# One core, one stream of tokens: the feed-forward layers with hi and lo of x in one 512-column product

## The chip, the cores and the metric

The program runs on one core of a Trainium2 chip. The metric is the device time of one execution in microseconds, the median of several. A core has five engines that work side by side: TensorE (PE) multiplies matrices, VectorE (DVE) and ScalarE (ACT) do element-wise work, GpSimd (POOL) does some more of it, and SyncE (SP) issues most DMA transfers. TensorE's clock has two levels, 1.2 and 2.4 GHz; the profile's "granted clock" is its share of the higher one.

## The reference

Two transformer blocks run one after the other on 256 tokens of width 1024, all in float32. Each has two layers. What the change touches are the feed-forward parts, four in block 1 and one or two in each layer of block 2:

```python
def rmsnorm(x, g):
    xf = x.astype(F32)
    y = xf * lax.rsqrt(jnp.mean(xf * xf, axis=-1, keepdims=True) + EPS)
    return (y * g.astype(F32)).astype(x.dtype)

def swiglu(x, w1, w3, w2):
    return (jax.nn.silu(x @ w1) * (x @ w3)) @ w2
...
        h = h + 0.5 * swiglu(rmsnorm(h, g[0]), ffn_w1[layer, 0], ffn_w3[layer, 0], ffn_w2[layer, 0])
...
        h = h + 0.5 * swiglu(rmsnorm(h, g[2]), ffn_w1[layer, 1], ffn_w3[layer, 1], ffn_w2[layer, 1])
```

w1 and w3 are 1024 x 2816, w2 is 2816 x 1024. Between the feed-forward parts stand an attention mixer per layer and, in block 2, vectors that modulate the activations (`w_mod`) and a second stream of 256 context tokens that lives through block 2's first layer.

## The kernel before

**Tiles.** Activations lie transposed: 128 of the 1024 features on the partitions, the 256 tokens along the free axis, so x is 8 blocks of 128x256 and a feed-forward's inner activation g is 22 such blocks (22 x 128 = 2816). One "weight block" is 128x128 numbers.

**Products.** A float32 product is made of three faster ones. Every operand v is kept as hi = v rounded to the type float32r and lo = v - hi, and `mm3` (L318) issues whi x xhi, whi x xlo and wlo x xhi (L324, L325, L326), each a TensorE product of 256 columns, all added up in PSUM. So a weight block of a one-stream feed-forward costs three products and three loads of weights. Where both streams of block 2 share the weights, the same three products have 512 columns.

**Weights.** All weights are one list of chunks of 8 blocks (128x1024, 512 KB). `Weights.prepare` (L274) splits a chunk: ScalarE writes hi (L279), VectorE lo (L280). SP loads chunks three ahead; four split chunks are held, so `block` (L285) has chunk h+3 split while chunk h is in use.

**A feed-forward of block 1** (`ffn1_layer`, L838, four times). The up stage has 22 steps j. A step multiplies x by block column j of w1 and of w3, 16 weight blocks or two chunks; both results, 128x256 each, lie in one PSUM bank, one of four (tag `mm`). A chunk holds, for four input blocks k, the blocks of w1 and w3 side by side. x there is h times the norm's gain g, without the norm's factor r = 1/sqrt(mean of squares), which comes later than x: VectorE multiplies the 128x512 result by r (L863), ScalarE takes silu of the first half (L865), VectorE multiplies by the second (L866), and `split` makes hi and lo of the product (L330 on ScalarE, L331 on VectorE). Then the down stage makes 8 output blocks m, each of 22 weight blocks, and VectorE adds half of each to h (L797; L817 in the last one), after which `rms_feed` prepares the next layer's x (L513, L514) and its squares.

**What runs beside it.** `step` lets background work advance once per j and per m. In the first three feed-forwards that is `mod_gen`, which computes the modulation vectors without TensorE: per step one pass over 128x1024 on VectorE (L724), one on ScalarE (L727) and one on GpSimd (L728). The first two also have `late_gen` and `later_gen`, which build small tables.

**Block 2.** `up_gen` (L1490) and `down_gen` (L1521) do the same with one or two streams. In layer 0 the first 6 of the 22 up steps run for each stream by itself, and the second half of the down stage runs stream by stream; layer 1 has one stream. There silu reads PSUM directly (L1508), VectorE multiplies (L1509), and L1543 adds to the residual.

**Order.** Each engine works through its own queue in order. The order is set when the program is built, by a scheduler that puts each engine's instructions where its own timeline has them ready; `issue_after` binds background work to marks.

## Time and profile before

| what | value |
|---|---|
| time, median of 3 runs | 2070.68 us (2070.18 to 2071.23) |
| the profiled execution: its own time | 2064.2 us |
| the profiled execution: span from first to last instruction | 2062.4 us |
| mean granted clock of TensorE | 0.990 |
| PE busy | 1999.6 us, 97% of the span, 15403 products |
| DVE busy | 1510.5 us, 73% |
| ACT busy | 1101.6 us, 53% |
| POOL busy | 401.7 us, 19% |
| DMA | 355.40 MB moved, 172 GB/s on the mean |

Busy time is the time in which at least one instruction of the engine was running. TensorE's products overlap: a product of 256 columns is listed with some 0.28 us though one starts every 0.12 us, so the distance from start to start says what one costs in a stream. The stages, read from where the products change from x to g as operand: the up stages of block 1's four feed-forwards run from 8.3 to 150.3, from about 346 to 485.4, from 548.8 to 681.5 and from about 826 to 953.7 us, and the down stages follow each up stage, to 222.7, 548.8, 745.0 and 1018.6 us. The one of block 2's layer 1 is the last part of the program: up to 1984.2, down to 2049.

### The profile page before, as it was taken

How to read it: one execution, taken by the hardware profiler on the slowest of the kernel's cores; microseconds unless marked ns; L12 is line 12 of the kernel's file. 1: busy time of each engine (PE TensorE's matmuls, PEld its weight loads, DVE VectorE, ACT ScalarE, POOL GpSimd, SP SyncE). 2: the span in 40 equal slices, each digit the busy share in tenths (PEclk: the TensorE clock that was granted, in tenths of full speed). 3: DMA queues.
4: the chain of work that ended last, by engine and by line, in shares of the span. 5: the costliest groups of instructions: out<-in, count | busy, mean ns of one | idle time of the engine just before them, and what ended most of it. 6: DMA issues, size and time to landing. Idle time of an engine off the chain costs nothing. (4 is left out here: it accounts for less than half of the span.)

```text
span 2062.4 us, 39061 instructions
## 1 busy us (share of the span) xinstructions
PE 1999.6 (97%) x15403; PEld 1857.6 (90%) x15403; DVE 1510.5 (73%) x2646; ACT 1101.6 (53%) x1908; POOL 401.7 (19%) x287
## 2 busy tenths in 40 slices
PE   8998999999999999999999999999999999989997
PEld 8988999999999998999998877988888889869997
DVE  6787797997599667886685877665664678776554
ACT  5465586655466457554545665533442455655443
POOL 1223141421043111210410012301330013002002
PEclk9999999999999999999999999999999999999999
DMA  6775645876576663555632323475555653124553
GB/s 223 256 263 181 204 141 185 300 240 219 180 245 215 195 205 123 184 174 184 191 123 72 105 68 118 144 243 165 168 161 162 222 166 108 50 82 156 184 182 103
DMA packets 117113, 355.40 MB, mean 172 GB/s; under 512 B 21781, under 2 KB 27624, under 8 KB 116480
## 3 DMA queue, kind: packets, MB, share of 16 engines
q1 hardware_dynamic: 115472, 344.54, 50.9%
q10 hardware_dynamic: 1456, 8.36, 1.1%
q8 instruction: 121, 1.98, 0.4%
q14 instruction: 64, 0.52, 0.1%
HBM read 351.66 MB, written 8.90 MB: 175 GB/s over the span
## 5 line engine op out<-in xcount | busy, mean ns | idle before, releaser
L280 DVE TENSOR_TENSOR wlo<-wst,whi 128x1024 fp32r<-128x1024 f32 x540 | 719.6, 1333 | 333.0 <-ACT whi L279 327.3
L324 PE MATMUL mm<-HI,whi 128*128 128x256 f32 (+1 forms) x2944 | 866.8, 297 | 13.7 <-ACT whi L279 8.3
L326 PE MATMUL mm<-HI,wlo 128*128 128x256 f32 (+1 forms) x2944 | 863.8, 294 | 4.8 <-DVE wlo L280 4.8
L325 PE MATMUL mm<-LO,whi 128*128 128x256 f32 (+1 forms) x2944 | 866.4, 295 | 1.5 <-DVE LO L1413 1.5
L279 ACT ACTIVATE whi<-wst 128x1024 fp32r<-128x1024 f32 x540 | 570.1, 1056 | 532.2 <-PE mm L325 298.7
L324 PEld LDWEIGHTS mm<-HI,whi 128*128 128x128 f32 x2944 | 564.4, 193 | 42.3 <-issue 15.1
L325 PEld LDWEIGHTS mm<-LO,whi 128*128 128x128 f32 x2944 | 567.2, 193 | 20.6 <-issue 7.9
L326 PEld LDWEIGHTS mm<-HI,wlo 128*128 128x128 f32 x2944 | 566.8, 193 | 19.0 <-DVE wlo L280 5.7
L326 PE MATMUL mm<-ghi,wlo 128*128 128x256 f32 (+1 forms) x1000 | 288.5, 289 | 3.5 <-DVE wlo L280 3.5
L324 PE MATMUL mm<-ghi,whi 128*128 128x256 f32 (+1 forms) x1000 | 287.2, 288 | 2.1 <-ACT ghi L330 2.1
L325 PE MATMUL mm<-glo,whi 128*128 128x256 f32 (+1 forms) x1000 | 288.2, 288 | 0.0
L728 POOL TENSOR_TENSOR macc<-macc,mp 128x1024 f32<-128x1024 f32 (+1 forms) x70 | 172.3, 2462 | 438.0 <-ACT mp L727 251.2
L326 PEld LDWEIGHTS mm<-ghi,wlo 128*128 128x128 f32 x1000 | 192.2, 192 | 7.2 <-DVE wlo L280 3.9
L324 PEld LDWEIGHTS mm<-ghi,whi 128*128 128x128 f32 x1000 | 191.6, 192 | 5.2 <-ACT ghi L330 2.3
L325 PEld LDWEIGHTS mm<-glo,whi 128*128 128x128 f32 x1000 | 192.2, 192 | 2.5 <-issue 1.1
L724 DVE SCALAR_TENSOR_TENSOR macc<-mw,sc,macc 128x512 f32<-128x512 f32 (+1 forms) x126 | 155.7, 1236 | 26.6 <-DMA mw<-in_wmod 20.2
L325 PE MATMUL mm<-wlo,HI 128*128 128x256 f32 x352 | 100.8, 287 | 3.4 <-DVE wlo L280 3.4
L324 PE MATMUL mm<-whi,HI 128*128 128x256 f32 x352 | 102.0, 290 | 0.0
L326 PE MATMUL mm<-whi,LO 128*128 128x256 f32 x352 | 99.9, 285 | 0.0
L727 ACT ACTIVATE mp<-mw,sc 128x1024 f32<-128x1024 f32 (+1 forms) x70 | 67.5, 974 | 30.3 <-DMA mw<-in_wmod 19.0
L330 ACT ACTIVATE ghi<-w 128x256 fp32r<-128x256 f32 (+1 forms) x120 | 51.2, 427 | 55.2 <-DVE w L866 54.4
L527 POOL TENSOR_TENSOR sacc<-sacc,w 128x256 f32<-128x256 f32 x36 | 33.6, 932 | 234.0 <-ACT w L523 227.8
(414 smaller groups left out, 2436.5 us busy)
## 6 DMA issues: line engine op xcount, KB each, us to landing
wst<-in_wall SPq DMA_DIRECT2D x540, 512.0 KB
mw<-in_wmod SPq DMA_DIRECT2D x48, 512.0 KB
mw<-in_wmod SPq DMA_DIRECT2D x96, 256.0 KB
brep<-bvec ACTq DMA_DIRECT2D x16, 384.0 KB
nab<-rrep SPq DMA_DIRECT2D x24, 96.0 KB
bias<-brep SPq DMA_DIRECT2D x4, 512.0 KB
bias<-brep SPq DMA_DIRECT2D x8, 256.0 KB
rrep<-in_rpb ACTq DMA_DIRECT2D x4, 348.8 KB
```

The source lines that it names most:

```text
L279: self.marks.append(self.nc.scalar.activation(hi, src, AF.Copy))
L280: self.nc.vector.tensor_tensor(lo, src, hi.bitcast(FT), op=OP.subtract)
L324: nc.tensor.matmul(ps, wh, xh, start=first, stop=False, skip_group_check=True)
L325: nc.tensor.matmul(ps, wh, xl, start=False, stop=False, skip_group_check=True)
L326: self.last = nc.tensor.matmul(ps, wl, xh, start=False, stop=last, skip_group_check=True)
L330: self.marks = [self.nc.scalar.activation(hi, src, AF.Copy), self.nc.vector.tensor_tensor(lo, src, hi.bitcast(FT), op=OP.subtract)]
L527: nc.gpsimd.tensor_tensor(st["acc"], st["acc"], sq, op=OP.add)
L724: nc.vector.scalar_tensor_tensor(acc[:, i], w, s, acc[:, i], op0=OP.mult, op1=OP.add)
L727: nc.scalar.activation(t, w, AF.Copy, scale=s)
L728: nc.gpsimd.tensor_tensor(acc[:, i], acc[:, i], t, op=OP.add)
```

## The change

It touches the feed-forwards, at those places where one stream is alone.

1. hi and lo of an activation lie side by side in one tile (`HL` for x, `ghl` for g), and hi and lo of a weight chunk in one tile `whl`.
2. `mm3` takes another way where the target is twice as wide as x's hi: wlo x xhi with 256 columns into the left half of a PSUM bank, then whi x (xhi, xlo) with 512 columns into the whole bank. The left half then holds two of the three products and the right half the third, and the two halves have to be added.
3. Each output block of the up stage takes a bank of its own (`wide`), and w1's and w3's block columns follow each other as one chunk each (`_ffn1s`). `joined` copies the right half to SBUF on ScalarE and adds the left half on VectorE. On the way down VectorE adds the two halves to the residual in two instructions instead of one.
4. In block 1 the factor r is multiplied into the result only in the steps 0 to 3. After the steps 1 and 2 four blocks each of the normed x (h times g times r, split into hi and lo) are written, and from step 4 on the products read these.

```diff
+def _ffn1s(w1, w3, j0, j1):
+    out = []
+    for j in range(j0, j1):
+        for w in (w1, w3):
+            out.append(w[:, j * 128:(j + 1) * 128].reshape(KB, 128, 128).transpose(1, 0, 2))
+    return out
...
+NORM = 3
...
-        hi = self.split.tile([128, 1024], FR, name="whi")
-        lo = self.split.tile([128, 1024], FR, name="wlo")
-        self.marks.append(self.nc.scalar.activation(hi, src, AF.Copy))
-        self.nc.vector.tensor_tensor(lo, src, hi.bitcast(FT), op=OP.subtract)
+        w = self.split.tile([128, 2, 1024], FR, name="whl")
+        self.marks.append(self.nc.scalar.activation(w[:, 0], src, AF.Copy))
+        self.nc.vector.tensor_tensor(w[:, 1], src, w[:, 0].bitcast(FT), op=OP.subtract)
...
     def mm3(self, ps, w, x, first, last, swap=False):
...
+        if len(ps.shape) == 2 and len(xh.shape) == 2 and ps.shape[1] == 2 * xh.shape[1]:
+            nc.tensor.matmul(ps[:, :S], wl, xh, start=first, stop=False, skip_group_check=True)
+            self.last = nc.tensor.matmul(ps.rearrange("p (h t) -> p h t", h=2), wh, x[2], start=False, stop=last,
+                                         skip_group_check=True)
+            return
...
+    def wide(self, x, n):
+        ps = self.ps("mm")
+        for k in range(n):
+            self.mm3(ps, self.W.block(self.wpos + k), self.at(x, k), k == 0, k == n - 1)
+        self.wpos += n
+        return ps
+
+    def joined(self, dst, ps):
+        c = self.w1()
+        self.nc.scalar.activation(c, ps[:, S:], AF.Copy)
+        self.nc.vector.tensor_tensor(dst, ps[:, :S], c, op=OP.add)
...
-                nc.vector.scalar_tensor_tensor(hm, ps, scale, hm, op0=OP.mult, op1=OP.add)
+                for c in (0, S):
+                    nc.vector.scalar_tensor_tensor(hm, ps[:, c:c + S], scale, hm, op0=OP.mult, op1=OP.add)
...
-            for j in range(FB):
-                ps, = self.slab_fm([st["hl"]])
...
-                t = self.w2()
-                nc.vector.tensor_tensor(t, ps, st["r"][:, None, :].to_broadcast([128, 2, S]), op=OP.mult)
-                sl = self.w1()
-                nc.scalar.activation(sl, t[:, 0], AF.Silu)
+            turns = {1: range(4), 2: range(4, KB)}
+            t = None
+            for j, c in [(j, c) for j in range(FB) for c in range(2)]:
+                ps = self.wide(st["hl"] if j <= NORM else y, KB)
...
+                if c == 0:
+                    t = self.w2()
+                self.joined(t[:, c], ps)
+                if j <= NORM:
+                    nc.vector.tensor_tensor(t[:, c], t[:, c], st["r"], op=OP.mult)
+                if c == 0:
+                    sl = self.w1()
+                    nc.scalar.activation(sl, t[:, 0], AF.Silu)
+                    continue
                 nc.vector.tensor_tensor(sl, sl, t[:, 1], op=OP.mult)
-                self.split(gh[:, j], gl[:, j], sl)
+                self.split(g[:, j, 0], g[:, j, 1], sl)
                 self.step()
+                for m in turns.get(j, ()):
+                    w = self.w1()
+                    nc.vector.scalar_tensor_tensor(w, self.h[:, m], g0[:, m:m + 1], st["r"], op0=OP.mult, op1=OP.mult)
+                    self.split(y[0][:, m], y[1][:, m], w)
...
             for m in range(KB):
-                ps = self.ps("mm")[:, :S]
-                for k in range(FB):
-                    self.mm3(ps, self.W.block(self.wpos + k), (gh[:, k], gl[:, k]), k == 0, k == FB - 1)
-                evict(m, ps)
-                self.wpos += FB
+                evict(m, self.wide(parts2(g), FB))
...
     def up_gen(self, js, streams, g, j0):
...
                 i = streams[0]
-                ps, = self.slab_fm([self.hl(1 - i)])
+                t = self.w2()
+                for c in range(2):
+                    self.joined(t[:, c], self.wide(self.hl(1 - i), KB))
                 sl = self.w1()
-                a, b = ps[:, 0], ps[:, 1]
+                a, b = t[:, 0], t[:, 1]
...
     def down_gen(self, streams, g, evict, nk=FB // 2):
...
+                if len(streams) == 1:
+                    self.mm3(ps, w, parts(g(k, streams[0])), k == 0, k == nk - 1)
+                    continue
...
-                nc.vector.scalar_tensor_tensor(R[:, m], ps, self.mod(l, i, 5, m), R[:, m], op0=OP.mult, op1=OP.add)
+                for c in range(0, ps.shape[1], S):
+                    nc.vector.scalar_tensor_tensor(R[:, m], ps[:, c:c + S], self.mod(l, i, 5, m), R[:, m],
+                                                   op0=OP.mult, op1=OP.add)
```

The new lines have numbers of their own in the built program: L350 and L351 are the two products, L369 and L370 the copy and the add of `joined`, L925 the multiplication by r, L935 the normed x, L379 and L380 the split, L930 the gate, L847 the residual, L297 the weights' lo, L773 the modulation pass.

TensorE, third feed-forward, from the end of the first step to the second. Before (mm_6736 and mm_6816 are the banks of steps 0 and 1, whi/wlo a chunk, st the sum of squares for r):

```order
L324 MATMUL mm_6736<-HI_82,whi_6661 128x256
L325 MATMUL mm_6736<-LO_83,whi_6661 128x256
L326 MATMUL mm_6736<-HI_82,wlo_6662 128x256
L534 MATMUL st_6797<-w1_6724,ones_95 128x256
L324 MATMUL mm_6816<-HI_82,whi_6691 128x256
L325 MATMUL mm_6816<-LO_83,whi_6691 128x256
L326 MATMUL mm_6816<-HI_82,wlo_6692 128x256
```

Now, at the last blocks k of the same layer's first outputs (mm_5867, mm_5902 and mm_5937 are three banks):

```order
L350 MATMUL mm_5867<-HL_82,whl_5781 128x256
L351 MATMUL mm_5902<-HL_82,whl_5810 128x512
L583 MATMUL st_5889<-w1_5856,ones_94 128x256
L350 MATMUL mm_5902<-HL_82,whl_5810 128x256
L350 MATMUL mm_5937<-HL_82,whl_5831 128x256
L351 MATMUL mm_5937<-HL_82,whl_5831 128x512
L351 MATMUL mm_5867<-HL_82,whl_5781 128x512
```

Two products stand for three, and the scheduler has the last blocks of three outputs side by side, so that the last blocks of x are wanted late.

VectorE, third feed-forward, one whole step j in the middle of the up stage, from one modulation pass to the next. Before:

```order
L724 SCALAR_TENSOR_TENSOR macc_6884<-mw_7105,sc_111,macc_6884 128x1024
L863 TENSOR_TENSOR w2_7394<-mm_7333,rstd_6800 128x512
L280 TENSOR_TENSOR wlo_7409<-wst_7294,whi_7408 128x1024
L866 TENSOR_TENSOR w1_7396<-w1_7396,w2_7394 128x256
L280 TENSOR_TENSOR wlo_7439<-wst_7338,whi_7438 128x1024
L331 TENSOR_TENSOR glo_6735<-w1_7396,ghi_6734 128x256
L724 SCALAR_TENSOR_TENSOR macc_6884<-mw_7179,sc_111,macc_6884 128x1024
```

Now:

```order
L773 SCALAR_TENSOR_TENSOR macc_5995<-mw_6154,sc_110,macc_5995 128x1024
L370 TENSOR_TENSOR w2_6430<-mm_6408,w1_6431 128x256
L930 TENSOR_TENSOR w1_6372<-w1_6372,w2_6368 128x256
L297 TENSOR_TENSOR whl_6437<-wst_6350,whl_6437 128x1024
L297 TENSOR_TENSOR whl_6471<-wst_6378,whl_6471 128x1024
L370 TENSOR_TENSOR w2_6430<-mm_6436,w1_6458 128x256
L380 TENSOR_TENSOR ghl_5866<-w1_6372,ghl_5866 128x256
L773 SCALAR_TENSOR_TENSOR macc_5995<-mw_6216,sc_110,macc_5995 128x1024
```

Two adds of 256 stand for one multiplication of 512; the rest is the same.

VectorE, third feed-forward, after the first gates. Before, the modulation passes begin there:

```order
L280 TENSOR_TENSOR wlo_6965<-wst_6851,whi_6964 128x1024
L866 TENSOR_TENSOR w1_6952<-w1_6952,w2_6950 128x256
L280 TENSOR_TENSOR wlo_6995<-wst_6894,whi_6994 128x1024
L331 TENSOR_TENSOR glo_6735<-w1_6952,ghi_6734 128x256
L724 SCALAR_TENSOR_TENSOR macc_6884<-mw_6812,sc_111,macc_6884 128x1024
L863 TENSOR_TENSOR w2_7024<-mm_6963,rstd_6800 128x512
```

Now the normed x stands there (w1_6004, w1_6008, w1_6012 are three of its eight blocks), and the modulation comes behind all eight:

```order
L925 TENSOR_TENSOR w2_5959<-w2_5959,rstd_5892 128x256
L935 SCALAR_TENSOR_TENSOR w1_6004<-h_83,vec_84,rstd_5892 128x256
L297 TENSOR_TENSOR whl_6046<-wst_5941,whl_6046 128x1024
L935 SCALAR_TENSOR_TENSOR w1_6008<-h_83,vec_84,rstd_5892 128x256
L935 SCALAR_TENSOR_TENSOR w1_6012<-h_83,vec_84,rstd_5892 128x256
L930 TENSOR_TENSOR w1_5964<-w1_5964,w2_5959 128x256
L380 TENSOR_TENSOR HL_82<-w1_6004,HL_82 128x256
L297 TENSOR_TENSOR whl_6097<-wst_5970,whl_6097 128x1024
L380 TENSOR_TENSOR HL_82<-w1_6008,HL_82 128x256
```

What moved: sixteen VectorE instructions and eight ScalarE ones came in ahead of the first modulation pass.

## Rows read from the trace of the kernel before

**Rows 1.** Products in the third up stage (start, duration in us, instruction): 85 in a row.

```profile
559.84 0.28 PE L325 MATMUL mm<-LO,whi 128*128 128x256 f32 x1
...
569.92 0.28 PE L325 MATMUL mm<-LO,whi 128*128 128x256 f32 x1
```

**Rows 2.** The same view, both streams of block 2 together: 90 in a row.

```profile
1479.80 0.39 PE L325 MATMUL mm<-LO,whi 128*128 128x512 f32 x1
...
1499.97 0.39 PE L324 MATMUL mm<-HI,whi 128*128 128x512 f32 x1
```

**Rows 3.** The same view, where products of both widths meet.

```profile
1417.08 0.28 PE L326 MATMUL mm<-ghix,wlo 128*128 128x256 f32 x1
1417.20 0.40 PE L324 MATMUL mm<-ghi,whi 128*128 128x512 f32 x1
...
1420.41 0.39 PE L326 MATMUL mm<-ghi,wlo 128*128 128x512 f32 x1
1420.64 0.28 PE L324 MATMUL mm<-early_qcT,whi 128*128 128x256 f32 x1
```

**Rows 4.** By stage: stretch, length, busy us (count) per engine, clock, DMA share, GB/s.

```profile
8.27:150.30 142.03, 137.26 (x1075) 132.04 (x1076) 112.38 (x125) 80.25 (x117) 29.57 (x15) 0.99 0.73 247
150.30:222.70 72.40, 66.79 (x538) 65.17 (x537) 55.41 (x48) 36.34 (x47) 23.09 (x12) 0.98 0.57 189
346.00:485.40 139.40, 134.97 (x1085) 131.70 (x1085) 129.38 (x182) 84.70 (x118) 44.39 (x20) 0.98 0.73 249
485.40:548.80 63.40, 63.40 (x531) 63.40 (x530) 36.87 (x40) 29.33 (x38) 5.57 (x6) 1.00 0.63 214
548.80:681.50 132.70, 131.96 (x1078) 128.09 (x1077) 117.82 (x122) 81.41 (x110) 45.52 (x14) 1.00 0.67 220
...
826.00:953.70 127.70, 127.70 (x1054) 126.95 (x1053) 102.17 (x147) 70.65 (x114) 19.59 (x18) 1.00 0.56 181
953.70:1018.60 64.90, 64.90 (x537) 64.34 (x535) 39.99 (x45) 32.88 (x48) 19.66 (x18) 1.00 0.56 181
1862.00:1984.20 122.20, 121.30 (x1009) 121.07 (x1009) 70.58 (x87) 60.47 (x92) 5.23 (x4) 1.00 0.55 181
1984.20:2049.00 64.80, 64.80 (x535) 64.06 (x534) 27.73 (x29) 23.50 (x29) 12.56 (x12) 1.00 0.41 139
```

**Rows 5.** VectorE through one step of the third up stage.

```profile
599.72 0.68 DVE L863 TENSOR_TENSOR w<-mm,rstd 128x512 f32<-128x512 f32 x1
600.32 2.83 DVE L280 TENSOR_TENSOR wlo<-wst,whi 128x1024 fp32r<-128x1024 f32 x1
603.07 0.41 DVE L866 TENSOR_TENSOR w<-w,w 128x256 f32<-128x256 f32 x1
603.41 1.21 DVE L280 TENSOR_TENSOR wlo<-wst,whi 128x1024 fp32r<-128x1024 f32 x1
604.54 0.41 DVE L331 TENSOR_TENSOR glo<-w,ghi 128x256 fp32r<-128x256 f32 x1
604.88 1.27 DVE L724 SCALAR_TENSOR_TENSOR macc<-mw,sc,macc 128x1024 f32<-128x1024 f32 x1
606.07 0.68 DVE L863 TENSOR_TENSOR w<-mm,rstd 128x512 f32<-128x512 f32 x1
```

**Rows 6.** GpSimd in the same stretch.

```profile
598.77 3.30 POOL L728 TENSOR_TENSOR macc<-macc,mp 128x1024 f32<-128x1024 f32 x1 [3.06 <-ACT mp L727]
```

**Rows 7.** Two groups: count, busy us, mean ns, then idle before and its enders.

```profile
L797 DVE SCALAR_TENSOR_TENSOR h<-mm,h 128x256 f32<-128x256 f32 x24 | 10.1, 421 | 10.3 <-PE mm L326 10.3
L976 ACT ACTIVATE HI<-half 128x256 fp32r<-128x256 f32 x16 | 6.1, 381 | 11.0 <-PE half L970 10.9
```

**Rows 8.** ScalarE near the start: the second of the two passes that make r.

```profile
24.59 0.42 ACT L549 ACTIVATE rstd<-rstd 128x256 f32<-128x256 f32 x1
```

**Rows 9.** VectorE in the first up stage: two results two steps apart.

```profile
96.97 0.68 DVE L863 TENSOR_TENSOR w<-mm,rstd 128x512 f32<-128x512 f32 x1
...
110.74 0.68 DVE L863 TENSOR_TENSOR w<-mm,rstd 128x512 f32<-128x512 f32 x1
```

155 lines of the change are left out of this document (83 added, 72 removed).

## The prediction

> **What bounds the kernel now.** I read the stages first, then the distances between products, then VectorE inside one stage. By stage [rows 4] TensorE is busy nearly all the time in every feed-forward: 63.40 of 63.40 us in the second down stage, 127.70 of 127.70 in the fourth up stage. Busy time alone says little, since products overlap, so the starts decide. In the third up stage 85 products of 256 columns start within 10.08 us [rows 1], which is 0.120 us each. A down stage of 176 weight blocks and three products each is then 528 x 0.120 = 63.4 us, just its length: TensorE issues without a pause there. An up stage of 352 blocks would be 126.7 us. The first three up stages take 142.0, 139.4 and 132.7 us [rows 4], so 15.3, 12.7 and 6.0 us more, and VectorE is the one that is short in them: 112.4, 129.4 and 117.8 us busy. One step shows why [rows 5]: from one result to the next VectorE needs 6.35 us, while TensorE needs 16 x 0.360 = 5.76 us. In it stands a weights' lo of 2.83 us where the next one takes 1.21, because GpSimd runs its 3.30 us pass at the time [rows 6] and VectorE's instruction ends only 1.1 us after that pass. In the first up stage a step takes 6.9 us (13.77 for two) [rows 9]. Only the steps without a modulation pass let VectorE catch up.
>
> **What TensorE gains.** Where both streams go through together, 90 products of 512 columns start within 20.17 us, 0.2266 each [rows 2]. Where the widths meet, a 512 follows a 256 after 0.12 and a 256 follows a 512 after 0.23 us [rows 3], so mixing them brings no extra cost that 10 ns can show. A block now takes 0.120 + 0.2266 = 0.3466 us instead of 0.360: 0.0134 us less, a price per product that stays when its columns double (0.120 less the 0.1067 of 256 columns at 2.4 GHz, 0.2266 less 0.2133: 0.0133 both times). The built program has 3008 such pairs of products: 5 x 528 for block 1's four feed-forwards and block 2's last, 368 in block 2's first layer. That is 3008 x 0.0134 = 40.3 us if TensorE set the pace everywhere; with the 0.35 of [rows 3] it would be 30. I take 0.0134, since it comes from long series. Per up stage it is 4.7, per down stage 2.4 us.
>
> The Trainium skill, "TensorE: Matmul & The Clock Gate", section "Back-to-back issue gap", gives the distance of isolated products at full clock as N/2.4 + 2.5 ns, so 109 and 216 ns. By that one product fewer is worth 2.5 ns, and the whole 7.5 us. The trace does not agree: 120 and 227 ns with a load of weights before each product.
>
> **What VectorE and ScalarE pay.** In an up stage of block 1 the 22 multiplications of 0.68 [rows 5] go, and 44 adds of one PSUM and one SBUF operand come, 0.42 each by the residual's group [rows 7]: 22 x (0.84 - 0.68) = +3.5 us. The eight multiplications by r in the steps 0 to 3 are +3.4 (8 x 0.42), the normed x is +6.7 (16 x 0.42). Together +13.6 us of VectorE per up stage. ScalarE gets 44 copies from PSUM of 0.38 [rows 7] and eight splits of 0.41, +20 us; with 80 to 85 of 133 to 142 us busy it has room, but the copies stand in one queue with the weights' hi. In the up stage of block 2's last feed-forward it is 44 adds more and nothing less, +18.5 us on VectorE's 70.6 of 122.2 [rows 4]: hidden. On the way down the second add to the residual is +3.4 us per stage beside 37 of 63: hidden.
>
> **The three up stages with modulation** are the open part. A step of the third goes from 6.35 to 6.35 + 2 x 0.34 - 0.60 = 6.43 us (distances of starts), and as the instruction behind the modulation pass is now an add of 0.34 where a multiplication of 0.60 ran beside GpSimd, up to 0.26 more: 6.4 to 6.7, against 5.55 for TensorE. Over 8 passes VectorE falls 7 to 9 us behind, gets some 4 back in the two steps between the two groups of passes, and falls behind again. TensorE can run ahead by what is prepared: three chunks (3 x 2.77 = 8.3 us), less now that one output fills a bank (4 x 2.77 instead of 4 x 5.76 us until a bank must be free) and that each copy holds one of four work buffers; I take 5. So I expect 3 to 10 us of waiting per stage. Third stage: 122.0 + some 2.5 for small products + 3 to 10 = 128 to 135, taken 131, +1.7 against 132.7. Second: its other 12.7 us (clock 0.98, chains of small tables) stay: 122.0 + 12.7 + 3 to 10, taken 141, -1.6. First: its 15 steps with passes are paced by VectorE already at 6.9, so TensorE's gain of 0.21 per step there goes (3.1), each gets 0.1 to 0.3 dearer (1 to 4), and r, ready at 25.0 [rows 8], now holds the second of four banks, where TensorE would come at 22 to 25: 1 to 3 us. Taken 145, -3.0. The floor of all three is the full gain, +4.7 each; the other end is that the 13.6 us come on top, each.
>
> The normed x itself costs less than it looks. From r to its last block stand some 20 VectorE instructions of 0.34 to 0.42 and six weights' lo of 1.21, some 17 us; in the third stage that ends about 25 us after the stage's start, when step 4 begins at 22.2. But the built order has the last blocks k of three outputs side by side, as at a layer's start, so the last block is wanted some 6 us into step 4. I charge 1.0 in the fourth stage (102.2 + 13.6 of 123 us busy) and have it in the ranges of the others.
>
> **The sum.** Three up stages -2.9 (loss). First down stage, still with passes, +0.5. Four down stages 4 x 2.4 = +9.6. Fourth up stage 4.7 - 1.0 = +3.7. Last up stage +4.1 (4.7 less 0.6 for longer chains). Block 2's first layer 368 x 0.0134 = 4.9, taken +3.1, as its first six steps run beside chains of small work. Second residual adds at the ends of layers, where the next operand waits for them, four times 0.34 to 0.42: -1.5. Sum: 16.6 us saved. The profiled execution of 2064.2 us (span 2062.4) would become 2047.6; the median of 2070.7 lies 6.5 above it and becomes 2054.
>
> **Rivals.** *Full cover*: VectorE's addition falls into its 10 to 30 idle us of the three stages and TensorE keeps its gain there: 19.5 for the rest + 14.1 = 33.6, 2037. For it: the normed x is made before the passes begin. Against it: 6.43 against 5.55 us per step. *VectorE takes over*: the place is again the three up stages. Each added instruction delays the lo of the next chunk, TensorE waits for it, and nothing catches up: 3 x 13.6 = 40.8 lost against 19.5 gained elsewhere, +21, 2092. It decides from 19.5 / 3 = 6.5 us per stage on, about half of the 13.6. For it: second stage, 129.4 + 13.6 = 143 us of VectorE in 139. Against it: VectorE idles 10 to 30 us per stage now and the down stages (37 of 63 busy) can take up arrears. *No gain per block*: the price per product belongs to something that the wide product pays twice, and 0.120 + 0.240 is the old 0.360. Then the second residual adds (1.5) and the three stages (2.9) are all that is left, +4.4, 2075. For it: the distance in mixed rows is read to 10 ns alone [rows 3]. Against it: 0.2266 over 90 products [rows 2].
>
> The page of the Trainium skill named above comes near that: by its 2.5 ns the 21 us of the stages that TensorE paces become 4, and the time some 2071.
>
> **How the numbers follow.** Forecast 0.62 (2044 to 2064 about 2054), full cover 0.13, a weaker form with 7 to 12 us more waiting in the three stages 0.11 (2062 to 2068), VectorE takes over 0.09, no gain per block 0.05. A run of this kernel can tell about 0.2% (4.1 us) from no change: 2066.5 to 2074.8. Faster: 0.62 + 0.13 + 0.07 of the weaker form; within: 0.04 of that, 0.04 of no gain per block and 0.02 of a half-way VectorE; slower: 0.07 + 0.01. The range of 2036 to 2070 leaves out most of the slower case and the ends.
>
> **What would show it.** Right: products 0.120 and 0.227 apart in the down stages, these at 61 us; the last up stage at some 118; up stages of 145, 141 and 131 with waits of TensorE for the weights' lo; steps with passes 6.4 to 6.7 us apart. Wrong: a down stage of 63 us (no gain per block); first three up stages under 125 or over 150; a wait of some us at step 4 for the normed x in every layer; or the clock at half after new waits, where each us loses half a us of products.

## The result, and the profile after

The changed kernel takes 2124.33 us (median, 2120.87 to 2127.51) against 2070.43 for the kernel before: 1.0263 times as long, with a 95% interval of 1.0249 to 1.0276. I had predicted 2054 us with a range of 2036 to 2070. The sign was wrong, by 70 us in all.

The profiled execution has a span of 2123.9 us and a mean granted clock of 0.978. By stage, with the columns of [rows 4] (first come the four pairs of up and down stages of block 1, then the part of block 2's first layer ahead of its first down stage, then the last up stage):

```profile
9.70:157.10 147.40, 135.45 (x724) 112.52 (x724) 120.83 (x168) 95.54 (x167) 33.18 (x15) 0.99 0.71 237
157.10:226.90 69.80, 64.51 (x362) 54.75 (x361) 56.81 (x56) 35.50 (x46) 21.02 (x11) 0.98 0.60 189
352.00:509.10 157.10, 138.37 (x735) 116.20 (x734) 142.04 (x225) 96.61 (x169) 46.13 (x20) 0.95 0.67 219
509.10:571.30 62.20, 62.20 (x355) 53.92 (x354) 40.88 (x51) 29.70 (x40) 6.09 (x6) 1.00 0.66 226
571.30:723.70 152.40, 136.15 (x726) 112.12 (x725) 136.99 (x170) 95.21 (x162) 35.13 (x14) 0.96 0.60 191
723.70:785.00 61.30, 61.30 (x356) 53.90 (x355) 39.86 (x53) 28.97 (x38) 6.13 (x6) 1.00 0.61 195
863.10:1012.40 149.30, 133.20 (x718) 113.58 (x717) 114.33 (x198) 88.81 (x172) 18.74 (x20) 0.95 0.48 157
1012.50:1074.40 61.90, 61.90 (x356) 53.94 (x355) 42.25 (x50) 31.75 (x46) 18.96 (x18) 1.00 0.57 188
1255.80:1476.30 220.50, 205.33 (x1244) 165.51 (x1244) 159.05 (x305) 119.90 (x241) 38.14 (x24) 0.97 0.43 140
1919.30:2046.30 127.00, 126.65 (x705) 109.59 (x705) 97.26 (x140) 76.57 (x143) 16.61 (x10) 0.98 0.55 174
```

The last two rows and that of the fourth up stage begin 352 weight blocks ahead of the down stage; by the same count they read in the kernel before:

```profile
824.00:953.70 129.70, 129.70 (x1071) 128.95 (x1070) 104.17 (x151) 72.65 (x120) 21.44 (x20) 1.00 0.56 181
1199.10:1413.30 214.20, 207.27 (x1438) 176.43 (x1437) 147.01 (x281) 113.01 (x217) 37.99 (x24) 0.98 0.44 144
1853.50:1984.20 130.70, 129.19 (x1057) 128.38 (x1057) 79.08 (x97) 63.98 (x100) 13.73 (x10) 0.99 0.52 170
```

So the five down stages became 1 to 3 us shorter each and the last up stage 3.7. The four up stages of block 1 became longer, by 5.4, 17.7, 19.7 and 19.6 us, and block 2's first layer by 6.3. The fourth up stage is the striking one: it has no modulation, VectorE is busy for 114 of its 149 us, and yet it lost as much as the others.

What TensorE waits for in the second up stage (who waits for whom: us in total, times, longest):

```profile
PE mm L350 <- DVE w L370: 12.6, 5, 3.5
PE mm L350 <- DVE whl L297: 5.5, 3, 3.4
PE mm L350 <- ACT HL L379: 0.6, 1, 0.6
```

and in the fourth, where the kernel before has no such line at all:

```profile
PE mm L350 <- DVE w L370: 14.8, 4, 6.0
PE mm L350 <- ACT xn L379: 0.8, 1, 0.8
PE mm L351 <- DVE xn L380: 0.2, 1, 0.2
```

L370 is the add that joins the two halves. When TensorE waits for it, it waits for a PSUM bank to be emptied. A long wait is mostly paid twice, since the granted clock falls to half for some us behind it. TensorE in the fourth up stage (start, duration, instruction):

```profile
913.40 0.39 PE L351 MATMUL mm<-xn,whl 128*128 128x512 f32 x1
916.73 0.55 PE L350 MATMUL mm<-xn,whl 128*128 128x256 f32 x1 [2.94 <-DVE w L370]
...
917.51 0.41 PE L350 MATMUL mm<-xn,whl 128*128 128x256 f32 x1
...
918.15 0.41 PE L350 MATMUL mm<-xn,whl 128*128 128x256 f32 x1
...
920.07 0.28 PE L350 MATMUL mm<-xn,whl 128*128 128x256 f32 x1
...
920.42 0.28 PE L350 MATMUL mm<-xn,whl 128*128 128x256 f32 x1
```

A gap of 3.3 us, then pairs 0.64 us apart (917.51 to 918.15), then again 0.35 (920.07 to 920.42). Put together for the fourth stage: 4.7 us gained by the products (its share in the prediction), 15.8 lost in the waits above, and 0.05 x 149.3 = 7.5 in the lower clock, +18.6 of the 19.6 that were measured (the clock's share is a little too large, since part of the half clock falls into the waits: 0.81 from 892.0 to 898.7 us). For the second stage: 4.7 gained, waits of 18.7 in place of 4.4, clock of 0.95 x 157.1 in place of 0.98 x 139.4 (7.9 less 2.8), +14.7 of 17.6.

Why an add comes so late shows in the fourth stage from 884 to 899 us. VectorE and ScalarE, the lines that matter (start, duration, engine, instruction, and in brackets the idle time before it):

```profile
884.71 0.36 ACT L369 ACTIVATE w<-mm 128x256 f32<-128x256 f32 x1
...
892.11 1.06 ACT L296 ACTIVATE whl<-wst 128x1024 fp32r<-128x1024 f32 x1 [1.71 <-PE mm L351]
893.07 0.36 ACT L1513 ACTIVATE w<-st 128x256 f32<-128x256 f32 x1
...
894.34 0.42 DVE L1516 TENSOR_TENSOR ex<-cx,w 128x256 f32<-128x256 f32 x1
894.68 0.87 DVE L935 SCALAR_TENSOR_TENSOR w<-h,vec,rstd 128x256 f32<-128x256 f32 x2
...
897.80 0.38 ACT L369 ACTIVATE w<-mm 128x256 f32<-128x256 f32 x1
898.21 0.42 DVE L370 TENSOR_TENSOR w<-mm,w 128x256 f32<-128x256 f32 x1
```

and TensorE at the same time:

```profile
892.05 0.70 PE L1511 MATMUL st<-sacc,ones 128*128 128x256 f32 x2
898.78 0.55 PE L350 MATMUL mm<-xn,whl 128*128 128x256 f32 x1 [6.04 <-DVE w L370]
```

Between 884.7 and 897.8 no result is copied out, 13 us, while TensorE finishes one every 2.77 us: the four banks are full and it stops. ScalarE is not overworked, it stands in its queue. The built program gives the reason (ScalarE's queue there; mm_9064 is the result whose copy comes last):

```
L296 ACTIVATE whl_9208<-wst_9097 128x1024
L1513 ACTIVATE w1_9043<-st_9041 128x256
L1255 ACTIVATE w1_9046<-ex_8977 128x256
L379 ACTIVATE xn_8911<-w1_9048 128x256
L379 ACTIVATE xn_8911<-w1_9052 128x256
L379 ACTIVATE xn_8911<-w1_9056 128x256
L379 ACTIVATE xn_8911<-w1_9060 128x256
L369 ACTIVATE w1_9087<-mm_9064 128x256
```

L1513 reads a small sum of the background work (st_9041), which TensorE makes behind all four results (892.05 us). The four buffers w1 serve all of this: w1_9043 is read by eight instructions through the steps that follow, and in the addresses of the built program the copy w1_9087 lies in the same buffer as w1_9048 and w1_9056, two blocks of the normed x. The copy stands behind their splits; in both queues these stand behind the background's turn (L1513, L1516), and that waits for TensorE.

### The profile page after: what moved, and what is told of

It reads as the page before. It is cut to its first block, busy times and chain, and to the rows that moved or that the text cites. A ratio compares the mean times of both kernels' runs of the same rounds, so it can differ in the third digit from the quotient of the medians.

```text
span 2123.9 us, 33702 instructions
## 1 busy us (share of the span) xinstructions
PE 2000.8 (94%) x12395; PEld 1706.4 (80%) x12395; DVE 1613.8 (76%) x2954; ACT 1180.5 (56%) x2184; POOL 398.9 (19%) x287
## 4 chain that ended last, share of the span: by engine, by line
PE 68%; DVE 17%; issue 6%; ACT 4%; DMA 4%; POOL 0%; ACTq 0%; DVEq 0%; SPq 0%; POOLq 0%
PE mm L351 22%; PE mm L350 12%; PE mm L354 8%; PE mm L355 8%; PE mm L356 8%; DVE whl L297 6%; DMA wst<-in_wall 3%; ACT whl L296 2%; PE sc L1668 2%; DVE macc L773 2%; DVE w L370 1%; PE half L1709 1%; PE tp L1697 1%; PE st L1355 1%; DVE w L930 1%
## 5 line engine op out<-in xcount | busy, mean ns | idle before, releaser
L297 DVE TENSOR_TENSOR whl<-wst,whl 128x1024 fp32r<-128x1024 f32 x540 | 692.9, 1285 | 255.3 <-ACT whl L296 252.5
L296 ACT ACTIVATE whl<-wst 128x1024 fp32r<-128x1024 f32 x540 | 569.0, 1056 | 408.7 <-PE mm L351 163.3
L351 PE MATMUL mm<-HL,whl 128*128 128x512 f32 x1664 | 604.3, 406 | 0.7 <-DVE HL L1477 0.6
L350 PE MATMUL mm<-HL,whl 128*128 128x256 f32 x1664 | 478.8, 290 | 56.2 <-DVE whl L297 26.0
L350 PEld LDWEIGHTS mm<-HL,whl 128*128 128x128 f32 x1664 | 324.5, 196 | 78.1 <-DVE whl L297 31.5
L351 PEld LDWEIGHTS mm<-HL,whl 128*128 128x128 f32 x1664 | 321.1, 194 | 78.8 <-issue 4.4
L351 PE MATMUL mm<-ghl,whl 128*128 128x512 f32 x960 | 339.3, 397 | 0.0
L354 PE MATMUL mm<-HL,whl 128*128 128x256 f32 (+1 forms) x992 | 306.7, 315 | 6.5 <-ACT whl L296 3.8
L355 PE MATMUL mm<-HL,whl 128*128 128x256 f32 (+1 forms) x992 | 309.1, 313 | 0.0
L356 PE MATMUL mm<-HL,whl 128*128 128x256 f32 (+1 forms) x992 | 307.6, 313 | 0.0
L350 PE MATMUL mm<-ghl,whl 128*128 128x256 f32 x960 | 270.2, 282 | 5.3 <-DVE whl L297 4.6
L351 PEld LDWEIGHTS mm<-ghl,whl 128*128 128x128 f32 x960 | 180.6, 188 | 43.8 <-issue 1.3
L354 PEld LDWEIGHTS mm<-HL,whl 128*128 128x128 f32 x992 | 186.5, 191 | 26.0 <-issue 7.1
L355 PEld LDWEIGHTS mm<-HL,whl 128*128 128x128 f32 x992 | 189.2, 191 | 15.3 <-issue 5.1
L356 PEld LDWEIGHTS mm<-HL,whl 128*128 128x128 f32 x992 | 188.5, 190 | 12.5 <-issue 2.2
L773 DVE SCALAR_TENSOR_TENSOR macc<-mw,sc,macc 128x512 f32<-128x512 f32 (+1 forms) x126 | 173.1, 1374 | 20.1 <-DMA mw<-in_wmod 17.1
L350 PEld LDWEIGHTS mm<-ghl,whl 128*128 128x128 f32 x960 | 181.5, 189 | 7.9 <-DVE whl L297 5.4
L370 DVE TENSOR_TENSOR w<-mm,w 128x256 f32<-128x256 f32 x244 | 100.1, 416 | 56.5 <-ACT w L369 55.6
L369 ACT ACTIVATE w<-mm 128x256 f32<-128x256 f32 x244 | 88.8, 373 | 96.1 <-PE mm L351 87.3
L351 PE MATMUL mm<-xn,whl 128*128 128x512 f32 x288 | 103.7, 404 | 0.2 <-DVE xn L380 0.2
```

Source lines behind the costliest of these rows:

```text
L296: self.marks.append(self.nc.scalar.activation(w[:, 0], src, AF.Copy))
L297: self.nc.vector.tensor_tensor(w[:, 1], src, w[:, 0].bitcast(FT), op=OP.subtract)
L350: nc.tensor.matmul(ps[:, :S], wl, xh, start=first, stop=False, skip_group_check=True)
L351: self.last = nc.tensor.matmul(ps.rearrange("p (h t) -> p h t", h=2), wh, x[2], start=False, stop=last, skip_group_check=True)
L354: nc.tensor.matmul(ps, wh, xh, start=first, stop=False, skip_group_check=True)
L355: nc.tensor.matmul(ps, wh, xl, start=False, stop=False, skip_group_check=True)
```

## The experiments

Lengths of the up stages of block 1, of the first-layer stretch of block 2 and of the last up stage, us, and the time. The profile of one execution stands behind each row, and single runs (e5 to e9, e11, e13, e14) have one time each. The profiled execution of the kernel before was one of 2064.2 us, so the differences of the stages add up to some 6 us more than those of the times. The same code has been seen with different lengths in the second up stage (146, 146 and 140 in e4, e10 and e12) and in the first (142.8 and 145.7 in e5 and e13); the third and fourth repeat within 1 us. So differences below 7 us in the second stage and below 3 in the first tell nothing. "No modulation" means that seven of eight modulation passes are left out: e11 and e14 do not compute the whole.

| kernel | up 1 | up 2 | up 3 | up 4 | block 2 | last up | time |
|---|---|---|---|---|---|---|---|
| before | 142 | 139 | 133 | 130 | 214 | 131 | 2070.4 |
| after | 148 | 157 | 152 | 149 | 221 | 127 | 2124.3 |
| e1 seven banks | 152 | 154 | 150 | 145 | 221 | 127 | 2121.6 |
| e2 no normed x | 154 | 161 | 146 | 147 | 222 | 127 | 2136.6 |
| e3 before, two banks | 146 | 145 | 133 | 130 | 215 | 131 | 2076.1 |
| e4 down stages only | 143 | 146 | 134 | 130 | 209 | 131 | 2063.6 |
| e5 own buffers | 143 | 151 | 143 | 139 | 221 | 127 | 2099.5 |
| e6 own buffers, seven banks | 148 | 151 | 149 | 141 | 222 | 125 | 2104.6 |
| e7 before + VectorE load | 143 | 143 | 147 | 130 | 212 | 131 | 2089.4 |
| e8 before + hop | 145 | 150 | 149 | 130 | 213 | 131 | 2095.9 |
| e9 own buffers, no normed x | 146 | 145 | 148 | 129 | 221 | 125 | 2094.0 |
| e11 own buffers, no modulation | 141 | 130 | 126 | 139 | 221 | 125 | 2046.1 |
| e14 no modulation | 149 | 132 | 129 | 149 | 221 | 127 | 2071.9 |
| e13 own buffers everywhere | 146 | 151 | 144 | 139 | 216 | 126 | 2094.7 |
| e12 down stages + last up | 142 | 140 | 134 | 130 | 209 | 127 | 2057.2 |
| e10 e12 + fourth up | 143 | 146 | 134 | 133 | 210 | 128 | 2061.4 |

My first theory (A) was the banks; its rivals were VectorE's amount of work (B), the burst of the normed x (C), then the shared work buffers (W) and the added hop over ScalarE (H).

### e1: seven banks

```diff
-        ps = self.ps("mm")
+        self.nring = getattr(self, "nring", -1) + ring
+        ps = self.ps("sc" if ring and self.nring % 7 > 3 else "mm")
...
-                ps = self.wide(st["hl"] if j <= NORM else y, KB)
+                ps = self.wide(st["hl"] if j <= NORM else y, KB, True)
```

> The changed kernel with seven PSUM banks in turn for the outputs of block 1's four up stages (four of the tag mm, three of sc) in place of four; nothing else differs. Theory A (banks): a bank now carries one output of 2.77 us where it carried two of 5.76 in all, so four banks let TensorE run 8.3 us past an output that waits to be copied out, where 17.3 were allowed before; copies that come 4 to 7 us late on the mean and up to 19 us late stop it. With seven banks it may run 16.6 us past: the waits for the copies and adds (5.4, 12.6, 4.7 and 14.8 us in the four stages) and most of the half-clock windows behind them go, the second to fourth up stage become 135 to 145, 130 to 138 and 124 to 130 us (from 157, 152, 149), and the time is 2065 to 2085. Theory B (VectorE has too much to do: +13.6 us per up stage): the banks only move the wait, the stages stay within 4 us, the time is 2115 to 2127.

Measured: 2121.55 us, 1.0238 of before (1.0217 to 1.0258). Theory A falls. In the first up stage the wait for the adds has gone, and the one for the weights' lo stands there instead:

```profile
PE mm L350 <- DVE whl L297: 19.6, 6, 9.5
```

The lo comes from the same VectorE queue. More banks let TensorE run on until the next thing from that queue is missing. The three added banks are those of the tag `sc`, in which the background's small sums lie too; whether this sharing took back a part of a gain was not tried.

### e2: no normed x

```diff
-                ps = self.wide(st["hl"] if j <= NORM else y, KB)
+                ps = self.wide(st["hl"], KB)
-                if j <= NORM:
+                if True:
-            turns = {1: range(4), 2: range(4, KB)}
+            turns = {}
```

> The changed kernel without the normed x: r is multiplied into the results of all 22 steps and the operand stays h times g. VectorE gets 36 multiplications of 0.42 more and 16 instructions of 0.42 less per up stage, +8.4 us net; ScalarE gets 8 splits less. Theory A (banks): the wait of 6.4 us at the fourth stage's step 4 goes, the other waits of 2 to 4 us for copies stay: 2105 to 2130. Theory B (amount of VectorE work decides): 3 to 4 stages each 8 us longer, 2140 to 2160. Theory C (the burst of normed x in steps 1 to 3 is what sets the stages back): the up stages fall by 10 us or more each, 2070 to 2090.

Measured: 2136.55 us, 1.0313 (1.0291 to 1.0334), between the expectations of A and B. The third and fourth stage fell by 6 and 2 us, the first and second rose. Inconclusive by itself: two effects of opposite sign, which e9 separates.

### e3: two banks in the kernel before

```diff
+        if name == "mm" and getattr(self, "ring", None) is not None:
+            return self.ring
...
+            ring = [self.ps("mm") for _ in range(2)]
             for j in range(FB):
+                self.ring = ring[j % 2]
                 ps, = self.slab_fm([st["hl"]])
+                self.ring = None
```

> The kernel before, with only two PSUM banks in turn for the results of block 1's up stages in place of four: TensorE may run 5.8 us past a result in place of 17.3. VectorE's and ScalarE's work is that of before. Theory A (banks): results are taken 4.2, 3.2, 2.6 and 0.8 us late on the mean in the four stages now, and 8 of them in the first and 3 in the second later than 5.5 us; these turn into waits and half-clock windows: the first stage 5 to 15 us longer, the second 3 to 8, the third 0 to 3, the fourth 0; 2078 to 2097. Theory B (VectorE's amount of work alone): unchanged, 2068 to 2074.

Measured: 2076.05 us, 1.0021 (1.0009 to 1.0033). The stages moved as A had it (+4, +6, +1, +1), less than it had it in all. Halving the banks costs 4 us here, where results are taken in time, and cannot account for 54.

### e4: down stages only

```diff
-            for j, c in [(j, c) for j in range(FB) for c in range(2)]:
-                ps = self.wide(st["hl"] if j <= NORM else y, KB)
+            for j, c in [(j, 1) for j in range(FB)]:
+                ps, = self.slab_fm([st["hl"]])
...
-                self.joined(t[:, c], ps)
...
+                nc.vector.tensor_tensor(t, ps, st["r"][:, None, :].to_broadcast([128, 2, S]), op=OP.mult)
```

and the up stages of block 2 and the order of their weights likewise as before.

> The wide product in the down stages and in block 2's other one-stream places on the way down only; the up stages as in the kernel before (three products of 256 columns, w1 and w3 in turns, one bank for two outputs, one multiplication by r of 512 columns, no normed x). All theories that put the loss into the up stages: block 1's up stages as before (142, 139, 133, 128 us), the down stages as in the changed kernel (70, 62, 61, 62 us), some 2 us won in each: 2057 to 2064. If the layout (hi and lo side by side in one tile, weights too) costs time by itself: up stages longer than before by 2 us or more each, 2068 or more.

Measured: 2063.64 us, 0.9963 (0.9945 to 0.9981): faster than the kernel before. The third and fourth up stage are back at 133.6 and 129.7 us, so the new layout of the tiles costs nothing that these stages show, and the down stages keep their gain.

### e5 and e6: own work buffers

```diff
-        c = self.w1()
+        c = self.own("wc")
...
-                    w = self.w1()
+                    w = self.own("wn")
```

where `own` takes one of four buffers of that name.

> The changed kernel with own work buffers in block 1's up stages: four for the copies of the right half (L369's w) and four for the normed x (L935's w), where both shared four (w1) with silu, gate, squares and the background's small sums. Theory W (work buffers): a copy must wait until VectorE or GpSimd has released the buffer four uses back, often one of the normed x or of a background sum, and so cannot take its bank in time; with own buffers the fourth up stage (149 us, no modulation there) falls to 125 to 135 and the second and third to 140 to 150: 2080 to 2105. Theory B (amount of VectorE work) and theory H (the way over ScalarE, whose queue stands behind the weights' hi): within 6 us of the changed kernel, 2115 to 2130.

Measured: 2099.45 us, some 25 less than the changed kernel; the four stages are shorter by 5, 6, 9 and 10. Theory W holds for about half of the loss; the fourth stage, at 139, stays above its 125 to 135. e6 adds the seven banks to it:

> Own work buffers as in e5 and seven PSUM banks as in e1 together. Theory W with banks as its second half: each alone leaves the other in the way, and both together let the copies and TensorE run free: fourth up stage 122 to 128 us, second and third 130 to 142, 2060 to 2080. Theories B and H: 2110 to 2130, the waits for the weights' lo of e1 (20, 12, 10 us in the first three up stages) stay.

Measured: 2104.64 us, no better than e5. Banks aren't what is short with own buffers either. What e5 has left in its third stage is the weights' lo, small waits all through it, at full clock:

```profile
PE mm L350 <- DVE whl L297: 10.3, 11, 1.8
```

### e7: VectorE's load alone

```diff
+            scr = mp.tile([128, S], FT, name="scr")
...
                 self.split(gh[:, j], gl[:, j], sl)
+                for _ in range(1 + j % 2):
+                    nc.vector.tensor_tensor(scr, sl, sl, op=OP.add)
```

> The kernel before, with 33 more VectorE instructions of 128x256 (0.42 us each, 13.9 us) per up stage of block 1, spread over the steps behind the split, on which nothing waits but the queue. Theory B (amount of VectorE work): the first three up stages 10 to 14 us longer each, with waits for the weights' lo, the fourth 0 to 5: 2100 to 2115. Theories W and H: VectorE's idle time takes most of it, 0 to 5 us per stage: 2070 to 2085.

Measured: 2089.37 us (the run of the kernel before beside it: 2075.04). Up stages two and three in the trace:

```profile
350.30:493.70 143.40, 133.72 (x1076) 130.24 (x1075) 135.71 (x188) 82.18 (x114) 43.25 (x20) 0.99 0.71 234
560.40:707.20 146.80, 133.15 (x1079) 129.23 (x1078) 136.58 (x154) 80.81 (x110) 34.57 (x14) 0.99 0.64 199
```

Neither expectation in full: 13.9 us of added work cost 1, 4, 14 and 0 us, and the down stages behind the first two became 3.6 and 3.4 us longer (76.2 and 66.9 us from their first product to the end of their last), so a part of the load is paid there. In the third stage, where VectorE reaches 136.6 of 146.8, theory B holds, though not one to one: VectorE's busy time grew there by 18.8 us, of which the added instructions are 13.0, and the modulation passes went from 1.43 to 3.11 us on the mean (e8 shows how that comes). In the fourth, where VectorE has room, the work is free.

### e8: the hop alone

```diff
+                tc = mp.tile([128, 2, S], FT, name="tc", bufs=2)
+                nc.scalar.activation(tc, ps, AF.Copy)
-                nc.vector.tensor_tensor(t, ps, st["r"][:, None, :].to_broadcast([128, 2, S]), op=OP.mult)
+                nc.vector.tensor_tensor(t, tc, st["r"][:, None, :].to_broadcast([128, 2, S]), op=OP.mult)
```

> The kernel before, with each result of block 1's up stages copied from PSUM to an own SBUF tile on ScalarE (128x512, an estimate of 0.6 us from the 0.38 of 256 columns) before VectorE multiplies it by r: one more hop between engines, no more instructions on VectorE, four banks for four results as before. Theory H (the hop): VectorE's multiplication waits for a copy that stands behind the weights' hi, and the lo of the weights queue behind it: each up stage 5 to 15 us longer, 2090 to 2120. Theories B and W: 2066 to 2076.

Measured: 2095.93 us: +3, +10, +16 and 0, of which most of the +10 can be the second stage's scatter. Without a single VectorE instruction more, the way over ScalarE costs no less than the load of e7, and only in stages with modulation. The time lies in the range of theory H, but the waits that it gave as the reason are not what the trace shows in the steps with passes. The third stage:

```profile
564.70:713.20 148.50, 137.17 (x1079) 129.41 (x1078) 126.07 (x123) 90.94 (x131) 37.16 (x14) 0.95 0.61 199
```

VectorE is busy for 126 of 148.5 us here, 8 more than in the kernel before. It also waits more for the weights' hi, which stands behind the copies in ScalarE's queue, 21.7 us in place of 11.5 (who waits for whom, same stretch):

```profile
DVE wlo L280 <- ACT whi L279: 21.7, 17, 2.7
```

These waits lie outside the steps with passes. In the first group of seven passes, 598.7 to 640.2 us, all that is left of them is this:

```profile
DVE wlo L280 <- ACT whi L279: 0.2, 1, 0.2
```

There VectorE works without a pause, and a step is longer (VectorE and GpSimd, one step of e8):

```profile
598.75 3.42 DVE L724 SCALAR_TENSOR_TENSOR macc<-mw,sc,macc 128x1024 f32<-128x1024 f32 x1
...
605.28 2.71 POOL L728 TENSOR_TENSOR macc<-macc,mp 128x1024 f32<-128x1024 f32 x1 [4.19 <-ACT mp L727]
605.64 3.42 DVE L724 SCALAR_TENSOR_TENSOR macc<-mw,sc,macc 128x1024 f32<-128x1024 f32 x1
```

From pass to pass it takes 6.89 us, where the kernel before takes 6.36 in most steps. VectorE's pass begins 0.36 us behind GpSimd's and is listed with 3.42 us. In the kernel before, VectorE's begins at 604.88 and takes 1.27 [rows 5]; GpSimd's follows 0.24 us later, and a lo behind it is the long one:

```profile
605.12 3.31 POOL L728 TENSOR_TENSOR macc<-macc,mp 128x1024 f32<-128x1024 f32 x1 [3.05 <-ACT mp L727]
```

So VectorE falls behind by some 0.5 us more per step, and TensorE waits for what comes out of its queue, here most of all for the modulation's sums and the lo:

```profile
PE st L736 <- DVE macc L724: 8.2, 2, 4.1
PE mm L326 <- DVE wlo L280: 3.1, 4, 0.9
```

How the 16 us divide between the longer steps and the waits for hi outside them was not taken apart. The changed kernel has the same long step in the second group of passes of its third stage, again without a pause of VectorE (6.95 us from pass to pass):

```profile
677.01 2.42 POOL L777 TENSOR_TENSOR macc<-macc,mp 128x1024 f32<-128x1024 f32 x1 [4.53 <-ACT mp L776]
677.10 3.43 DVE L773 SCALAR_TENSOR_TENSOR macc<-mw,sc,macc 128x1024 f32<-128x1024 f32 x1
...
684.05 3.43 DVE L773 SCALAR_TENSOR_TENSOR macc<-mw,sc,macc 128x1024 f32<-128x1024 f32 x1
```

No run moves GpSimd's passes alone, so the amount of VectorE's work and this stretching are not separated.

### e9 and e11: what is left with own buffers

e9 is e5 with the edit of e2. e11 is e5 with this edit in the modulation's loop:

```diff
                 for i in range(n):
+                    if l == 0 and k:
+                        continue
```

> Own work buffers as in e5, and without the normed x: r is multiplied into all results, as in e2. Against e5 VectorE has 8.4 us more per up stage, but no burst of 24 instructions in the steps 1 to 3. Burst theory: the wait of 8.1 us that e5 has left in the fourth up stage (for the copy and add that stand behind the normed x) is the burst's, so that stage falls from 139 to 122 to 130 us, while the second and third, where VectorE's amount of work sets the pace, get 3 to 8 us longer (151, 143 to 154 to 159, 146 to 151): 2085 to 2105. Amount theory alone: the fourth stage too gets longer, 140 to 147, and all is at 2110 to 2125.

Measured: 2094.03 us. The fourth stage, e5 first, then e9:

```profile
845.90:984.80 138.90, 128.97 (x718) 111.22 (x717) 114.39 (x198) 86.98 (x172) 19.15 (x20) 0.96 0.52 169
```

```profile
853.60:982.50 128.90, 127.18 (x719) 110.05 (x718) 115.15 (x209) 83.52 (x161) 21.82 (x20) 1.00 0.56 178
```

Ten us less, with slightly more work on VectorE and the clock at 1.00. The burst theory holds there. The third stage became 5 us longer, as expected of the 8.4 us of added multiplications; the second became 6 shorter, which is within its scatter.

> Own work buffers as in e5, and seven of eight of block 1's modulation passes left out (VectorE's, ScalarE's and GpSimd's; the output is not the reference's, and the loads of their weights stay). Amount theory: what the second and third up stages lose beyond the work buffers comes from VectorE, which with the passes has 135 to 139 us to do in 143 to 151: without them both stages fall by 10 us or more, to the fourth stage's 139 or below (125 to 140), and the first to 130 to 140: 2055 to 2080. If the chain of hops alone sets the pace of the steps, passes or none: second and third within 4 us of e5's 151 and 143, 2090 to 2100.

Measured: 2046.14 us, below the range of either theory. The second and third stage:

```profile
337.90:467.80 129.90, 127.80 (x734) 109.52 (x733) 103.35 (x215) 84.39 (x156) 4.30 (x6) 1.00 0.78 267
529.80:656.10 126.30, 126.30 (x725) 108.69 (x724) 96.34 (x157) 81.63 (x148) 0.00 (x0) 1.00 0.58 188
```

Both fall by 17 to 21 us, the third to 126.3 with TensorE busy throughout: where VectorE has 96 us to do in place of 135, the wide product, the hop and the normed x all fit. GpSimd's passes are gone there too, so this is the price of the passes as a whole. The fourth, which has no modulation, stays at 138.9 as it should.

### e14 and e13: two questions left open

> The changed kernel with seven of eight of block 1's modulation passes left out as in e11 (the output is not the reference's), but with the work buffers shared as in the changed kernel. It tells whether the shared buffers cost by themselves or only where VectorE is late. By themselves: the second and third up stages some 6 and 9 us above e11's 130 and 126 (the difference between the changed kernel and e5), 2060 to 2075. Only where VectorE is late: second and third within 3 us of e11's, the fourth at the changed kernel's 149 (it has the burst), 2050 to 2060.

Measured: 2071.86 us. Against e11 the shared buffers cost 2 us in the second and third stage, 10 in the fourth, and 8 in the first. In the time that is 26 us, as much as with the passes (25, e5). So they cost without a late VectorE too; in the second and third stage (6 and 9 with the passes) most of their price goes with the passes. Why the first pays 8 was not taken apart.

e13 is e5 and gives block 2's copies two buffers of their own.

> As e5, and two work buffers of their own for the copies in block 2's one-stream up stages, too. The stretch of block 2's first layer that has the wide ups (from the 352nd block before the two-stream down stage on) takes 221 us in the changed kernel and in e9 and e11, 209 with narrow ups (e4, e12), 214 in the kernel before. If the shared buffers are the cause there too, it falls to 209 to 215, and the time to 2085 to 2094; if it is VectorE's added adds and the copies beside that layer's chains of small work, it stays at 218 to 224, and the time at 2095 to 2103.

Measured: 2094.69 us; the stretch went from 221 to 216 us. That is 5 of the 12 us between the wide and the narrow ups. What the rest is was not taken apart.

### e12 and e10: towards a faster kernel

e12 is e4 with the wide up stage in the program's last feed-forward (`self.lastup = l == 1`, asked for in `up_gen`).

> The wide product in the down stages (e4) and in the last up stage of the program, where no background work runs beside and the changed kernel needed 127 us for the 352 blocks against 131 before. All theories: 3 to 4 us less than e4: 2056 to 2062 and 0.992 to 0.996 of the kernel before.

Measured: 2057.15 us, 0.9934 of the kernel before (0.9909 to 0.996), the fastest of those that compute the whole: the wide product where VectorE has room. e10 adds the fourth up stage, with own buffers and the normed x over four steps (`turns = {1: (0, 1), 2: (2, 3), 3: (4, 5), 4: (6, 7)}`).

> As e12, and the wide product in the fourth up stage of block 1 too, with own work buffers and the normed x spread over four steps (two blocks each after the steps 1 to 4, read from step 6 on). Burst theory: without the burst and without shared buffers the fourth stage, which has no modulation, keeps its gain: 124 to 127 us in place of 129.7, 3 to 6 us less than e12, 2051 to 2058. Amount theory: VectorE's 102 us there become 117 of 125, and the stage stays at 128 to 135: no gain over e12, or up to 5 us more.

Measured: 2061.43 us, 0.9952 (0.9935 to 0.9968). The fourth stage took 133 us, not 125: spreading the burst took 6 us off e5's 139, and left waits of 2.9 us for an add and 1.8 for the background's sum:

```profile
PE mm L350 <- DVE w L377: 2.9, 1, 2.9
PE st L1546 <- DVE sacc L1544: 1.8, 1, 1.8
```

That is what the amount theory had (128 to 135, no gain over e12), with VectorE busy for 117 us. But e9 ran this stage in 129 us with 115 us of VectorE, so what holds it in e10 stays open.

## Why the prediction was wrong

**The product's price was right.** In the third down stage 30 pairs lie between these two starts:

```profile
749.64 0.39 PE L351 MATMUL mm<-ghl,whl 128*128 128x512 f32 x1
...
760.04 0.39 PE L351 MATMUL mm<-ghl,whl 128*128 128x512 f32 x1
```

10.40 / 30 = 0.3467 us, where I had 0.3466. By the formula for isolated products in "TensorE: Matmul & The Clock Gate" of the Trainium skill, section "Back-to-back issue gap", a pair would be, as an estimate, 0.325; this stream, with a load of weights before each product, again does not run at it. From their first product to the end of their last, the five down stages gained 2.6, 1.2, 2.2, 1.9 and 1.2 us, some 9.0 in place of the 10.1 of the sum; the last up stage 3.7 in place of 4.1. (Its forecast of 118 us belonged to a stretch that began 8.5 us late; over all 352 blocks it is 126.6, and 127.0 came.) The small "no gain per block" rival is out.

**The normed x was mis-sized: 1.0 us in the fourth stage.** What it costs there hangs on the work buffers: with own buffers 10 us come back when it goes (139 to 129, e5 and e9), with the shared ones only 2 (149 to 147, e2). Own buffers alone give 10 (e5), both together 20. I had asked only when its last block is wanted. I had not asked what stands behind its 24 instructions on VectorE and ScalarE: the copies and adds that empty the banks. I named "a wait of some us at step 4 for the normed x in every layer" as a sign of error; what came was a wait for the banks, behind the normed x.

**The work buffers were named and not priced.** "each copy holds one of four work buffers; I take 5" took the effect as a shorter run-ahead of 5 us. By e5 it is some 25 us in the program, by e14 against e11 as much without the passes. Which other tiles share a ring, and how long the slowest of them holds its buffer, was to be read from the code: one background tile keeps its buffer through eight later reads.

**VectorE's step was mis-sized.** For the third stage I had 6.4 to 6.7 us from pass to pass, with the pass at its old 1.27. In the second group of passes it is 6.95, with the pass at 3.43 beside GpSimd's. VectorE falls 1.4 us per step behind TensorE's 5.55 there, where I had 0.9 to 1.1.

**The hop had no term at all.** I added up busy time: +13.6 us for VectorE, room for ScalarE's +20. e8 shows 16 us lost in the third stage from copies on ScalarE alone. They need no VectorE instruction more, but they shift the order in time, so that VectorE's passes run into GpSimd's and its steps go from 6.36 to 6.89 us. A short instruction on an engine with room isn't free if it shifts what a fuller engine does beside a third one.

**The three stages with modulation went the rival's way.** "VectorE takes over", 3 x 13.6, had 0.09. e7 and e11 show that VectorE sets the pace there: 14 us for 13.9 of added work in the third stage, and 17 to 21 us back when the modulation goes. My 3 to 10 us of new waiting per stage were some 14 and 16 in the second and third (18.7 and 16.3, with 4.4 and 0.7 before). In the first, the waits came to 21.3 us in place of 13.1. The catching up that I counted on is not free: in e7 the third stage lost all of its load, and the first two passed a part of it on to their down stages, which became 3.6 and 3.4 us longer. But the rival was too small as well, because it had neither the hop nor the buffers, and gave the fourth stage nothing.

**The clock stood under the signs and not in the sum.** The granted clock in the second to fourth stage fell from 0.98, 1.00 and 1.00 [rows 4] to 0.95, 0.96 and 0.95: that is at most 5.1, 6.1 and 7.5 us on top of the waits that led to it (the share below full clock times the length, less the same for the kernel before).

**Block 2's first layer** was forecast 3.1 us shorter and came 6.3 longer. Narrow ups there give 209 us (e4, e12), wide ones 221, own buffers 216. The sign is shown, the cause in half. That the stretch with narrow ups is some 3 to 6 us shorter than with the code of the kernel before (212 to 215), though its products are the same, stays unexplained.

What the page "Perfetto Trace Analysis" of the Trainium skill says in "Optimization Strategy", that a gap which keeps coming back on the engine that should be saturated can mean too few buffers for the next tile, fits e5 for the work buffers in SBUF; for the banks of PSUM, where the gap itself pointed, e1 does not bear it out. Its section "Identifying the Most-Contended Engine" advises to optimize the engine with the highest occupancy first, and to judge TensorE by the share of its peak that it reaches and the busy share of its weight loads, not by the busy share of its products. By the weight loads, too, TensorE came first: they are busy for 90% of the span of the kernel before, VectorE for 73%. Relieving it at VectorE's cost lost 54 us all the same. In two of the stages VectorE stood at 89 to 93% itself [rows 4], which the mean does not show, and the fourth, with VectorE at 80%, lost as much through the buffers and the normed x.

## What to carry to other kernels

Before a change that splits one eviction into several, list by stage how near the evicting engines are to full, and what shares their queues and their buffers; a sum of busy times prices none of this. A wait for a bank tells where TensorE stops, not what is short: follow the late instruction back through its queue and its buffer before adding banks. And apply such a change stage by stage: here the same edit was worth 1 to 3 us in a down stage and 4 in the last up stage, and cost 5 to 20 in the four up stages of block 1, in the fourth of which VectorE had room.

## What the runs showed of the hardware

The half-clock stretches set in behind gaps of TensorE that are short against the stage: behind the 3.3 us at 913.4, pairs went from 0.347 to 0.64 us and the granted clock was 0.50 until some 920.0, where it came back to 1.00. Not every such gap does it: behind one of 3.2 us at 935.3, in the same stage, the clock stayed at 1.00.

That GpSimd's passes stretch what VectorE does beside them was in the rows before; new was that it hits the small instructions just as much. A subtraction of 128x256, 0.42 us elsewhere, was listed with 2.30 us beside a pass of 2.69:

```profile
409.15 2.69 POOL L777 TENSOR_TENSOR macc<-macc,mp 128x1024 f32<-128x1024 f32 x1 [2.14 <-ACT mp L776]
...
409.82 2.30 DVE L380 TENSOR_TENSOR ghl<-w,ghl 128x256 fp32r<-128x256 f32 x1
```

Which VectorE instruction becomes long is a matter of the order: in the kernel before it was the lo of a chunk [rows 5, 6], in e8 and in the third stage of the changed kernel the modulation pass.
